# Attention, gate and hyena products in a fixed order on TensorE, with one bank for the projection and three for transposes and values

## The chip, the cores and the metric

The kernel runs on one core of a Trainium2 chip. The metric is the time of one execution in microseconds (us), the median of the runs shown. TensorE (PE) multiplies matrices into PSUM, which has 8 banks of 512 fp32 columns per partition. VectorE (DVE) and ScalarE (ACT) do the elementwise work, each in the order of its queue. SyncE (SP) and GpSimd (POOL) issue most DMAs.

## The reference

One layer of a diffusion backbone on 1024 tokens of width 1024, with 256 context tokens. One projection feeds two mixers, a neighbourhood attention (8 heads of 64) and a Hyena long convolution; their outputs are merged through sigmoid gates. Then come an output projection, a gated residual and a SwiGLU FFN. All six gates and shifts come from one vector (adaLN).

```python
h = modulate(rmsnorm(x, norm1_g[i]), sh1, sc1)
q, k, v, hv, hx1, hx2, gna, ghy = jnp.split(h @ w_in[i], IN_SPLITS, axis=-1)
y_na = neighbourhood_attention(to_heads(q), to_heads(k), to_heads(v), to_heads(k_c), to_heads(v_c), na_rpb[i])
y_hy = hyena_mixer(hv, hx1, hx2, *hy_params)
x = x + g1 * gated_merge(gna, ghy, y_na, y_hy, w_na_o[i], w_hy_o[i], w_out[i])
h2 = modulate(rmsnorm(x, norm2_g[i]), sh2, sc2)
x = x + g2 * swiglu(h2, ffn_w1[i], ffn_w3[i], ffn_w2[i])
# gated_merge:  m = sigmoid(g_na) * (y_na @ w_na_o) + sigmoid(g_hy) * (y_hy @ w_hy_o);  m @ w_out
```

Attention takes, for each query, a window of 8 rows by 16 columns of the 16 x 64 grid and all context keys, with a relative-position bias.

## The kernel before, in words

Products that need fp32 precision are made of three fp32r products: each operand is split into a high part (a cast, L174 on ACT) and a low part (a subtraction, L175 on DVE), and `gemm` (L186) adds low x high, high x low and high x high over the chunks of the contraction.

**The projection.** `project` (L552) makes the 40 chunks of `h @ w_in`, each of 128 output columns. A chunk has two halves of 512 tokens, a half is 24 matmuls of 128x512 into a tile in_ps (L560), so there are 80 halves. The last 16 chunks are the gates: ACT evicts each half with a sigmoid (L593) and POOL stores the chunk (L610). The weights of the next chunk are loaded and split ahead (wr, wh, wl).

**The convolution** runs beside the projection. Its last step transposes the result on PE in groups of four (yh_ps, L533; one bank, one buffer), ACT copies each group to yhT (L534), and POOL stores it.

**The attention** starts when the convolution is done (`self.fine`, L920). It has 32 items: a pair of heads, half the rows, a quarter of the columns. For an item:
- `scores` (L702): 12 matmuls into two tiles s_ps of two banks (two buffers), with operands krh, krl, kch, kcl, qh, ql, qrh, qrl. DVE adds the bias and takes the maximum (L728) into s, ACT makes the exponential into pe with its sum (L730), DVE takes the reciprocal and scales (L733, L734).
- `turn` (L737): five transposes of pe on PE into a tile pt_ps of two banks (L740), and a copy of 640 columns to pts by ACT (L742). An item calls it twice, once a head.
- `values` (L745): ten matmuls of v with pts into the unused columns of the pt_ps tile of the first head (L752), and a copy of 128 columns to yrow (L757).

An item's `turn` comes one step after its scores, its `values` two steps after. `keys` (L671) and `queries` (L693) load and prepare the operands of a pair: loads on SP (kraw, qraw, kcraw), a shuffle and rotary products on DVE, casts on ACT and subtractions on DVE. They are called in bursts at steps 1, 3 and 5 of the eight steps of a pair.

**Order.** Nothing here is pinned to program order: a scheduler places each instruction on its engine by its own estimate of when it is ready, and the generators' merge (`_merged`, with ATT1 = 23 steps of the attention beside the rest of the projection) only sets the order in which they are written. A half is written in three pieces (k 0-2, 3-5, 6-7) so that attention can come between. in_ps has two banks, in turn. PSUM: two banks in_ps, four s_ps, two pt_ps.

**After the last half** the projection's banks become ps1 (two banks), which hy_ps and al_ps share. `hyena_out` (L797) loads the convolution's result (yhraw, eight loads into two buffers), splits it (yhh, yhl), and makes 16 halves of 12 matmuls (hy_ps). DVE multiplies each by the stored gate (ghy, L816, in the buffers that yhraw used). `ada_late` (L836) sums the adaLN parts on PE (al_ps) from loads acc. Attention goes on beside them. Then `mix` begins with the attention's output product (na_ps).

Of the kernel before, what the change touches and what calls it, by code (L numbers as in the profile page):

```python
# [18 lines left out]
P = 128  # L19
D = 1024  # L20
T = 1024
# [3 lines left out]
ATT1 = 23  # L25
# [133 lines left out]
class Block:  # L159
# [26 lines left out]
    def gemm(self, ps, w, x, nk, width=512, pos=0, ks=None):  # L186

        nc = self.nc
        (wh, wl), (xh, xl) = w, x
        for k in ks or range(nk):  # L190
            for i, (ww, xx) in enumerate(((wl, xh), (wh, xl), (wh, xh))):
                nc.tensor.matmul(ps, ww[:, k * P:(k + 1) * P], xx[:, k, pos:pos + width],  # L192
                                 start=(k == 0 and i == 0), stop=(k == nk - 1 and i == 2))
# [358 lines left out]
    def project(self, groups, wpool, psg, psc, hT, hcT, between):  # L552

        nc = self.nc
        chunks = [f for g in groups for f in g]
        turn = []

        def half(f, w, st, ps, h):
            sl = slice(h * 512, (h + 1) * 512)
            pt = psg.tile([P, 512], F32, tag="g", name="in_ps")  # L560
            ps.append(pt)
            if self.fine:
                for ks in ((0, 1, 2), (3, 4, 5)):
                    self.gemm(pt, w, hT, 8, 512, h * 512, ks)
                    yield
                self.gemm(pt, w, hT, 8, 512, h * 512, (6, 7))
            else:
                self.gemm(pt, w, hT, 8, 512, h * 512)
# [50 lines left out]
        for group in groups:  # L619
# [7 lines left out]
            for h in range(2):  # L627
                for f, w, st, ps in zip(group, ws, sts, pss):
                    yield from half(f, w, st, ps, h)
# [11 lines left out]
    def attention(self, pool, kpool, prep, pss, pst):  # L641

        nc, a = self.nc, self.a
        rope = [kpool.tile([P, T], F32, name=f"rope{j}") for j in range(2)]
# [3 lines left out]
        nbias = 3  # L648
# [22 lines left out]
        def keys(pr):  # L671
# [9 lines left out]
            tl = {"v": v, "vc": vc, "q": [], "qr": []}  # L681
# [5 lines left out]
            for h in range(2):  # L687
                sl = slice(512 * h, 512 * h + 512)
                _, x = turned("k", self.qkd[4 + pr], sl, False)
                self.split(tl["kr"][0][:, sl], tl["kr"][1][:, sl], x)  # L690
            tiles[pr] = tl

        def queries(pr, h):  # L693

            for nm, x in zip(("q", "qr"), turned("q", self.qkd[pr], slice(512 * h, 512 * h + 512), True)):
                q = [prep.tile([P, 512], F32R, tag=nm + n, name=nm + n, bufs=2) for n in "hl"]
                self.split(*q, x)
                tiles[pr][nm].append(q)

        grid = lambda t, b: t[b:b + 64].rearrange("p (r c) -> p r c", c=64)  # L700

        def scores(it, pr, rb, cb):  # L702
# [15 lines left out]
            for i, (qq, kk) in enumerate(order):  # L718
                for ps, _, qs, _, kw, _ in halves:
                    nc.tensor.matmul(ps[:, 512:896], qs[qq], kw[kk], start=(i == 0), stop=(i == 2))  # L720
            for i, (qq, kk) in enumerate(order):
                for ps, _, _, qc, _, kc in halves:
                    nc.tensor.matmul(ps[:, 256:512], qc[qq], kc[kk], start=(i == 0), stop=(i == 2))  # L723
            pes = []
            for ps, bt, *_ in halves:
                s = pool.tile([P, 640], F32, tag="s", name="s", bufs=2)
                mx = pool.tile([P, 4], F32, tag="mx", name="mx", bufs=8)
                nc.vector.tensor_tensor_reduce(s, ps[:, 256:896], bt, -1.0, 3e38, ALU.add, ALU.min, mx[:, 0:1])  # L728
                pe = pool.tile([P, 640], F32, tag="pe", name="pe", bufs=4)
                nc.scalar.activation(pe, s, AF.Exp, bias=mx[:, 0:1], scale=-1.0, accum_out=mx[:, 1:2])  # L730
# [6 lines left out]
        def turn(pe):  # L737
            pt = pst.tile([P, T], F32, tag="t", name="pt_ps")
            for c in range(5):
                nc.tensor.transpose(pt[:, c * P:(c + 1) * P], pe[:, c * P:(c + 1) * P], self.ident)  # L740
            pts = pool.tile([P, 640], F32, tag="pts", name="pts", bufs=3)
            nc.scalar.copy(pts, pt[:, 0:640])  # L742
            return pts, pt

        def values(pts, yp, pr, rb, cb):  # L745

            tl = tiles[pr]
            for c in range(5):
                vv = tl["vc"][:, c, :] if c < 2 else tl["v"][:, 4 * (rb + c - 2) + cb, :]
                for hh in range(2):  # L750
                    ch = slice(64 * hh, 64 * hh + 64)
                    nc.tensor.matmul(yp[ch, 640:768], vv[:, ch], pts[hh][:, c * P:(c + 1) * P], start=(c == 0),  # L752
                                     stop=(c == 4), tile_position=(0, 64 * hh))
# [3 lines left out]
            nc.scalar.copy(dst, yp[:, 640:768].rearrange("p (r c) -> p r c", c=16))  # L757

        items = [(pr, rb, cb) for pr in range(4) for rb in range(2) for cb in range(4)]
        keys(0)  # L760
        queries(0, 0)
        yield
        one, two = {}, {}
        for it in range(len(items) + 2):
            if it < len(items):
                pr, at = it // 8, it % 8
                one[it] = scores(it, *items[it])
                if at == 1:
                    queries(pr, 1)
                elif at == 3 and pr < 3:  # L770
                    keys(pr + 1)
                elif at == 5 and pr < 3:
                    queries(pr + 1, 0)
            p0, p1 = one.pop(it - 1, (None, None))
            if p0 is not None:
                pts, yp = turn(p0)
                two[it - 1] = [pts]
            else:
                yp = pst.tile([P, T], F32, tag="t", name="pt_ps")
# [3 lines left out]
            if p1 is not None:  # L783
                two[it - 1].append(turn(p1)[0])
# [12 lines left out]
    def hyena_out(self, pool, wo, ps1):  # L797
# [10 lines left out]
        for f in range(8):  # L808
            w = self.weights(wo, a["why"][f], 512, "wf")
            for h in range(2):  # L810
                sl = slice(h * 512, (h + 1) * 512)
                ps = ps1.tile([P, 512], F32, tag="f", name="hy_ps")
                self.gemm(ps, w, yh, 4, 512, h * 512)
# [22 lines left out]
    def ada_late(self, pool, psf, part, gate):  # L836

        nc = self.nc
        for h in range(2):
            sl = slice(h * 512, (h + 1) * 512)  # L840
            acc = pool.tile([P, 512], F32, tag="acc", name="acc")
            nc.sync.dma_start(acc, self.accd[part][:, sl])
            ps = psf.tile([P, 512], F32, tag="f", name="al_ps")
            if gate is not None:
# [547 lines left out]
```

## Time and profile before

| | us |
|---|---|
| median of 3 runs (lowest, highest) | 1765.49 (1762.91, 1771.47) |
| the profiled execution | 1768.11 |
| its span | 1766.3 |
| mean granted clock of TensorE | 0.979 |
| first scores of the attention | 687.21 |
| last half of the projection ends, next item's scores | 848.32 |
| first matmul of na_ps | 965.26 |

The span runs from the first to the last instruction of the profiled execution. A row of a timeline has the start, the duration, engine, line and operation, the tiles written and read, the shapes, and in brackets how long the engine idled before it and what it waited for. The durations of matmuls overlap on PE, so a matmul's cost is read from start to start. "<-issue" is a wait that the profile names no releaser for. The clock column is 1.00 at full speed and 0.50 at half.

### The profile page before, as it was taken

The numbers are of one execution on the slowest core, as the hardware profiler recorded it, in microseconds if no ns is written. First come the engines' busy times: TensorE is split into PE (matmuls) and PEld (weight loads), VectorE is DVE, ScalarE is ACT, GpSimd is POOL, SyncE is SP. The second block draws the span as 40 slices with busy tenths as digits, with TensorE's granted clock in tenths as the row PEclk, the third lists the DMA queues.
The fourth block names the chain that finished last, engine by engine and source line by source line (L and its number), as shares of the span: only waits on it lengthen the run. The fifth ranks groups of instructions, "written<-read, shape, count | busy, mean of one in ns | idle before, by whom it ended". The sixth has DMA issues, their size and how long they took to land.

```text
span 1766.3 us, 22607 instructions
## 1 busy us (share of the span) xinstructions
PE 1687.7 (96%) x8128; PEld 1325.4 (75%) x8128; DVE 1226.2 (69%) x2040; ACT 693.0 (39%) x1190; POOL 142.8 (8%) x250
## 2 busy tenths in 40 slices
PE   6999899999999998999999999899999999999997
PEld 2777676777777776777677788688888888878886
DVE  4587487799797856856645867887656656469466
ACT  4611122312212124777734214633334333344555
POOL 0000010101100014022000000001100000100000
PEclk8999999999999998999999999999999999999999
DMA  8276756645455338444556624242322332395344
GB/s 339 106 245 196 233 191 209 224 143 182 137 205 184 135 120 212 122 141 124 171 181 202 228 77 167 92 153 103 135 92 90 102 107 96 112 370 167 101 120 150
DMA packets 111469, 285.36 MB, mean 162 GB/s; under 512 B 14707, under 2 KB 23543, under 8 KB 109053
## 3 DMA queue, kind: packets, MB, share of 16 engines
q1 hardware_dynamic: 91888, 221.32, 38.4%
q0 software_dynamic: 18816, 62.14, 10.2%
q8 instruction: 65, 1.06, 0.3%
q10 hardware_dynamic: 653, 0.44, 0.1%
q14 instruction: 47, 0.39, 0.1%
HBM read 213.86 MB, written 69.99 MB: 161 GB/s over the span
## 4 chain that ended last, share of the span: by engine, by line
PE 54%; issue 26%; DMA 8%; DVE 6%; ACT 2%; POOL 2%; SPq 0%; POOLq 0%; DVEq 0%; ACTq 0%
PE in_ps L192 18%; PE dx_ps L1261 6%; PE dft_ps L420 4%; PE out_ps L1041 3%; PE dz_ps L1261 3%; PE x_ps L1103 2%; DMA wal<-in_w_ada 2%; PE dft_ps L421 2%; PE dft_ps L422 2%; PE na_ps L192 2%; PE hy_ps L192 2%; PE pt_ps L752 2%; PE dy_ps L1261 2%; PE pt_ps L740 2%; POOL g L1214 1%
## 5 line engine op out<-in xcount | busy, mean ns | idle before, releaser
L192 PE MATMUL in_ps<-hTh,wl 128*128 128x512 f32 x640 | 260.4, 408 | 0.0
L192 PE MATMUL in_ps<-hTl,wh 128*128 128x512 f32 x640 | 255.7, 400 | 0.0
L192 PE MATMUL in_ps<-hTh,wh 128*128 128x512 f32 x640 | 254.3, 398 | 0.0
L192 PEld LDWEIGHTS in_ps<-hTl,wh 128*128 128x128 f32 x640 | 121.9, 191 | 27.3 <-issue 3.7
L192 PEld LDWEIGHTS in_ps<-hTh,wl 128*128 128x128 f32 x640 | 122.0, 191 | 26.0 <-issue 1.3
L192 PEld LDWEIGHTS in_ps<-hTh,wh 128*128 128x128 f32 x640 | 122.0, 191 | 25.9 <-issue 0.8
L175 DVE TENSOR_TENSOR ol<-ws,oh 128x512 fp32r<-128x512 f32 x88 | 60.2, 688 | 58.4 <-ACT oh L174 58.3
L174 ACT CAST wh<-wr 128x1024 fp32r<-128x1024 f32 x40 | 41.9, 1049 | 117.1 <-PE in_ps L192 88.3
L175 DVE TENSOR_TENSOR ol<-ar,oh 128x512 fp32r<-128x512 f32 x77 | 52.9, 687 | 46.1 <-ACT oh L174 46.1
L175 DVE TENSOR_TENSOR wl<-wr,wh 128x1024 fp32r<-128x1024 f32 x40 | 48.8, 1220 | 46.0 <-ACT wh L174 45.9
L174 ACT CAST oh<-ar 128x512 fp32r<-128x512 f32 x77 | 47.9, 622 | 81.8 <-PE dx_ps L1261 36.3
L420 PE MATMUL dft_ps<-a,matf 128*128 128x512 f32 x128 | 66.5, 601 | 7.1 <-issue 3.7
L174 ACT CAST oh<-ws 128x512 fp32r<-128x512 f32 x88 | 54.3, 622 | 47.7 <-PE x_ps L1103 16.4
L1261 PE MATMUL dx_ps<-ol,oh 128*128 128x512 f32 x176 | 69.6, 396 | 1.7 <-DVE ol L175 1.7
L1261 PE MATMUL dx_ps<-oh,ol 128*128 128x512 f32 x176 | 67.5, 392 | 3.7 <-ACT oh L174 3.5
L832 DVE SCALAR_TENSOR_TENSOR aacc<-wal,cs,aacc 128x1024 f32<-128x1024 f32 x32 | 41.0, 1282 | 41.9 <-DMA wal<-in_w_ada 41.0
L1261 PE MATMUL dx_ps<-oh 128*128 128x512 f32 x176 | 69.5, 395 | 0.0
L728 DVE CUSTOM_DVE_ANT_0 s<-s_ps,bias 128x640 f32<-128x640 f32 x64 | 50.6, 819 | 25.0 <-PE s_ps L723 24.9
L174 ACT CAST oh<-wr 128x512 fp32r<-128x512 f32 x70 | 43.2, 621 | 53.2 <-PE y_ps L1103 18.2
L175 DVE TENSOR_TENSOR ol<-wr,oh 128x512 fp32r<-128x512 f32 x70 | 48.0, 688 | 23.0 <-ACT oh L174 22.9
L742 ACT COPY pts<-pt_ps 128x640 f32<-128x640 f32 x64 | 44.2, 691 | 48.0 <-PE pt_ps L740 47.2
L1043 DVE TENSOR_TENSOR x<-x,out_ps 128x512 f32<-128x512 f32 x64 | 42.6, 684 | 19.3 <-PE out_ps L1041 18.9
(390 smaller groups left out, 4312.9 us busy)
## 6 DMA issues: line engine op xcount, KB each, us to landing
wr<-in_w SPq DMA_DIRECT2D x50, 512.0 KB, 3.3
wr<-in_w_in SPq DMA_DIRECT2D x40, 512.0 KB, 4.3
ar<-g SPq DMA_DIRECT2D x77, 256.0 KB, 2.9
wal<-in_w_ada SPq DMA_DIRECT2D x32, 512.0 KB, 4.1
g<-t POOLq DMA_DIRECT2D x49, 256.0 KB, 3.1
matf<-in_dft_f SPq DMA_DIRECT2D x32, 384.0 KB, 4.7
bias<-in_rpb SPq DMA_DIRECT2D x64, 192.0 KB, 2.9
w<-in_w SPq DMA_DIRECT2D x44, 256.0 KB, 5.4
```

What stands on the lines that cost most here:

```text
L174: self.nc.scalar.copy(hi, src)
L175: self.nc.vector.tensor_sub(lo, src, hi.bitcast(F32))
L192: nc.tensor.matmul(ps, ww[:, k * P:(k + 1) * P], xx[:, k, pos:pos + width], start=(k == 0 and i == 0), stop=(k == nk - 1 and i == 2))
L420: nc.tensor.matmul(ps, m[:, 0], v.rearrange("p a b -> p (a b)"), start=True, stop=False)
L421: nc.tensor.matmul(ps[:, 0:256], m[:, 1], v[:, 1], start=False, stop=False)
L422: nc.tensor.matmul(ps[:, 256:512], m[:, 2], v[:, 0], start=False, stop=True)
L728: nc.vector.tensor_tensor_reduce(s, ps[:, 256:896], bt, -1.0, 3e38, ALU.add, ALU.min, mx[:, 0:1])
L742: nc.scalar.copy(pts, pt[:, 0:640])
L832: nc.vector.scalar_tensor_tensor(acc, w, self.cs[:, 2 * k:2 * k + 1], acc, op0=ALU.mult, op1=ALU.add)
L1041: nc.tensor.matmul(ps, gg[x][:, tk], ww[y][:, sl], start=(i == 0), stop=(i == n - 1))
L1043: nc.vector.tensor_add(x1[:, sl], x1[:, sl], ps)
L1261: nc.tensor.matmul(ps[j], x[u][:, j * P:(j + 1) * P], w[v], start=(start and i == 0 and c == 0), stop=(stop and i == N - 1 and k == len(re ...
```

## The change

It sets the order of PE's instructions in this stage by hand and moves buffers and banks accordingly.

- `gemm` takes `pin`; with it every matmul keeps its place in program order (`keep_in_program_order`). The halves of the projection in this stage, scores, transposes of pe, values, hyena halves and al_ps are all pinned.
- A half is written in one piece. in_ps has two pools of one bank each, and in this stage only the first is used: one bank. The bank that is saved goes to pt_ps, which now has three banks and one buffer: ten transposes in columns 0 to 1279, values in 1280 to 1407. One copy of 1280 columns replaces two of 640.
- A step is written as scores of item i, ten transposes of item i-1, values of item i-2. Five units of the projection stand ahead of the first step, then one step and one half in turn.
- `operands()` prepares one piece (a quarter or so of a pair's operands) at every step, not in bursts. Bias tiles: four, not three. The reduction writes straight into pe, and the exponential is in place.
- After the last half: ps1 has one bank, hy_ps is pinned, `ada_late` is one generator over the parts 3, 4, 2, 5, and the steps of attention, hyena and al are interleaved by the step's number.

```diff
-    def gemm(self, ps, w, x, nk, width=512, pos=0, ks=None):
+    def gemm(self, ps, w, x, nk, width=512, pos=0, pin=False):
...
+                if pin:
+                    self.tc.keep_in_program_order(mm)
...
-            pt = psg.tile([P, 512], F32, tag="g", name="in_ps")
+            pt = psg[0 if self.fine else count[0] % 2].tile([P, 512], F32, tag="g", name="in_ps")
             ps.append(pt)
-            if self.fine:
-                for ks in ((0, 1, 2), (3, 4, 5)):
-                    self.gemm(pt, w, hT, 8, 512, h * 512, ks)
-                    yield
-                self.gemm(pt, w, hT, 8, 512, h * 512, (6, 7))
-            else:
-                self.gemm(pt, w, hT, 8, 512, h * 512)
+            self.gemm(pt, w, hT, 8, 512, h * 512, self.fine)
...
+        def operands():
+
+            values_of(0)
+            yield from keys(0)
+            yield from queries(0, 0)
+            for pr in range(4):
+                yield from queries(pr, 1)
+                if pr < 3:
+                    values_of(pr + 1)
+                    yield from keys(pr + 1)
+                    yield from queries(pr + 1, 0)
...
-                s = pool.tile([P, 640], F32, tag="s", name="s", bufs=2)
+                pe = pool.tile([P, 640], F32, tag="pe", name="pe", bufs=4)
...
-                nc.vector.tensor_tensor_reduce(s, ps[:, 256:896], bt, -1.0, 3e38, ALU.add, ALU.min, mx[:, 0:1])
...
+                nc.vector.tensor_tensor_reduce(pe, ps[:, 256:896], bt, -1.0, 3e38, ALU.add, ALU.min, mx[:, 0:1])
+                nc.scalar.activation(pe, pe, AF.Exp, bias=mx[:, 0:1], scale=-1.0, accum_out=mx[:, 1:2])
...
+        def turn(pes, pt):
+            for n, pe in enumerate(pes):
+                for c in range(5):
+                    at = 640 * n + c * P
+                    pin(nc.tensor.transpose(pt[:, at:at + P], pe[:, c * P:(c + 1) * P], self.ident))
+            pts = pool.tile([P, 2, 640], F32, tag="pts", name="pts", bufs=2)
+            nc.scalar.copy(pts.rearrange("p a b -> p (a b)"), pt[:, 0:1280])
+            return pts
...
+            pt = pst.tile([P, 1536], F32, tag="t", name="pt_ps")
+            if it - 1 in one:
+                two[it - 1] = turn(one.pop(it - 1), pt)
             if it >= 2:
-                values(two.pop(it - 2), yp, *items[it - 2])
+                values(two.pop(it - 2), pt, *items[it - 2])
...
-                for _ in _merged((proj, 6 * self.left), (attention, ATT1)):
-                    if not self.left:
-                        break
+                next(attention)
+                for _ in range(AHEAD):
+                    next(proj)
+                while self.left:
+                    next(attention)
+                    next(proj)
...
-                    ps1 = E4(tc.tile_pool(name="ps1", bufs=2, space=PSUM))
+                    ps1 = E4(tc.tile_pool(name="ps1", bufs=1, space=PSUM))
...
+                    for n, _ in enumerate(attention):
+                        if n > 2 and n % 4 != 3 or n in (3, 19):
+                            next(hyena, None)
+                        if n % 2:
+                            next(late, None)
```

What this does to the order, at three places. The first is ACT's queue from the convolution's last copy (yhT) into the attention. Each proj<-in_ps is the eviction of one half; kch, krh, qh and qrh are casts of the attention's operands, wh one of weights. Before:

```order
L534 COPY yhT_4956<-yh_ps_4963 128x512
L593 ACTIVATE proj_4977<-in_ps_4978 128x512
L174 CAST kch_5047<-kcraw_5045 128x256
L174 CAST wh_5151<-wr_5149 128x1024
L593 ACTIVATE proj_4977<-in_ps_5091 128x512
L174 CAST krh_5043<-kraw_5051 128x512
L593 ACTIVATE proj_5155<-in_ps_5156 128x512
L174 CAST krh_5043<-kraw_5060 128x512
L174 CAST qh_5073<-qraw_5069 128x512
```

After, from the same place:

```order
L539 COPY yhT_4959<-yh_ps_4966 128x512
L174 CAST kch_5060<-kcraw_5058 128x256
L594 ACTIVATE proj_4980<-in_ps_4981 128x512
L174 CAST krh_5056<-kraw_5064 128x512
L174 CAST wh_5126<-wr_5124 128x1024
L174 CAST krh_5056<-kraw_5073 128x512
L174 CAST qh_5086<-qraw_5082 128x512
L594 ACTIVATE proj_4980<-in_ps_5097 128x512
L174 CAST qrh_5093<-qraw_5082 128x512
L174 CAST qh_5276<-qraw_5272 128x512
L594 ACTIVATE proj_5130<-in_ps_5131 128x512
```

The evictions of the first two halves, which stood ahead of kch and of both krh, now stand behind kch and behind both krh and qh. Further on, not shown, the fourth half's follows kch, qrh and wh, and the fifth's two krh of the next pair.

The second place is PE in the middle of the attention. Before, one item's scores with what stands between them (in_ps the projection, pt_ps from ident the transposes, from v and vc the values):

```order
L192 MATMUL in_ps<-hTh,wh 128x512
L720 MATMUL s_ps<-krh,qrl 128x384 x2
L720 MATMUL s_ps<-krl,qrh 128x384 x2
L720 MATMUL s_ps<-krh,qrh 128x384 x2
L752 MATMUL pt_ps<-pts,vc 64x128 x4
L752 MATMUL pt_ps<-pts,v 64x128 x6
L723 MATMUL s_ps<-kch,ql 128x256 x2
L723 MATMUL s_ps<-kcl,qh 128x256 x2
L740 MATMUL pt_ps<-ident,pe 128x128 x5
L723 MATMUL s_ps<-kch,qh 128x256 x2
L192 MATMUL in_ps<-hTh,wl 128x512
```

After, an item there:

```order
L194 MATMUL in_ps<-hTh,wh 128x512
L739 MATMUL s_ps<-krh,qrl 128x384 x2
L739 MATMUL s_ps<-krl,qrh 128x384 x2
L739 MATMUL s_ps<-krh,qrh 128x384 x2
L742 MATMUL s_ps<-kch,ql 128x256 x2
L742 MATMUL s_ps<-kcl,qh 128x256 x2
L742 MATMUL s_ps<-kch,qh 128x256 x2
L759 MATMUL pt_ps<-ident,pe 128x128 x10
L771 MATMUL pt_ps<-pts,vc 64x128 x4
L771 MATMUL pt_ps<-pts,v 64x128 x6
L194 MATMUL in_ps<-hTh,wl 128x512
```

The item is one block, and the next rows are the 24 matmuls of a half without a break. From the first scores to the last projection matmul PE changes between projection, scores, transposes and values 145 times before and 44 times after; from there to na_ps 98 and 86 times (hyena and al counted as kinds as well). In the first of these stretches stand 320 projection matmuls, 21 items' scores, 200 transposes and 190 value matmuls before, and 288, 12, 110 and 100 after; what is missing there comes in the second, where before has 11 items' scores, 120 transposes and 130 value matmuls, and after 20, 210 and 220. Ahead of the first scores, the sixteen transposes yh_ps follow each other without a break after; before, 13, 4 and 4 projection matmuls stood between their groups. Behind them come 144 projection matmuls after, 90 before.

The third place is ACT behind the last half's eviction. Before, up to the second yhh (the cast of the convolution's result from its load yhraw):

```order
L730 ACTIVATE pe_7041,mx_7039<-s_7038,mx_7039 128x640
L730 ACTIVATE pe_7046,mx_7044<-s_7043,mx_7044 128x640
L757 COPY yrow_6734<-pt_ps_7067 128x8x16
L174 CAST yah_6977<-yrow_5291 128x512
L174 CAST yah_6977<-yrow_6013 128x512 x2
L174 CAST yah_6977<-yrow_6734 128x512
L174 CAST yhh_6988<-yhraw_6990 128x512
L174 CAST yhh_6988<-yhraw_6994 128x512
```

After:

```order
L761 COPY pts_6420<-pt_ps_6409 128x1280
L174 CAST wfh_6625<-wfr_6623 128x512
L174 CAST wfh_6794<-wfr_6792 128x512
L174 CAST yhh_6343<-yhraw_6345 128x512
L174 CAST yhh_6343<-yhraw_6349 128x512
L776 COPY yrow_6203<-pt_ps_6409 128x8x16
L748 ACTIVATE pe_6453,mx_6454<-pe_6453,mx_6454 128x640
L174 CAST yhh_6343<-yhraw_6353 128x512
L174 CAST yhh_6343<-yhraw_6357 128x512
```

The first yrow copy in this stretch stood ahead of the first yhh and now stands behind two of them; the next ones (not shown) stand behind the sixth and the eighth. On PE, al_ps follows directly behind a hyena half at the steps 3, 5, 9 and 13 behind the last half.

More of the change, by code (lines that the diff above doesn't have):

```diff
@@ L735, in scores, with values @@
             return [pe for pe, _ in pes]
[L737 to L745, printed above, removed]
+        def turn(pes, pt):
[6 more added lines that the diff above has]
+            return pts
+        def values(pts, pt, pr, rb, cb):
             tl = tiles[pr]
@@ L756, in values @@
             dst = self.yrow[pr].rearrange("p (r c) -> p r c", c=64)[:, 8 * rb:8 * rb + 8, 16 * cb:16 * cb + 16]
[L757 removed]
+            nc.scalar.copy(dst, pt[:, 1280:1408].rearrange("p (r c) -> p r c", c=16))
         items = [(pr, rb, cb) for pr in range(4) for rb in range(2) for cb in range(4)]
[L760 to L761 removed]
+        prepared = operands()
+        for _ in range(6):
+            next(prepared)
         yield
```

124 lines of the change are left out of this document (62 added, 62 removed).

## The prediction

> **What bounds the kernel now.** I read the page's head first, then busy time by stage, then what TensorE (PE) waits for in the stage that the change rewrites, then single instructions of that stage.
>
> ```profile
> span 1766.3 us, 22607 instructions
> PE 1687.7 (96%) x8128; PEld 1325.4 (75%) x8128; DVE 1226.2 (69%) x2040; ACT 693.0 (39%) x1190; POOL 142.8 (8%) x250
> ```
>
> The profiled execution took 1768.11 us, 2.6 above the median of the three timed runs (1765.49). PE is busy for 96% of the span, so two things can shorten the kernel: fewer PE microseconds, or less of the little idle time. The instructions up to the last transform of the convolution (641 us) and those from the mixing stage on (965.3 us, the first na_ps) stand in the same order on PE in both kernels. I therefore work on the 324 us between, in three pieces.
>
> ```profile
> 641.00:688.00 47.00, 39.55 (x183) 32.16 (x183) 29.24 (x47) 12.36 (x20) 15.30 (x28) 0.95 0.70 203
> 688.00:850.00 162.00, 160.20 (x1167) 123.48 (x1164) 108.92 (x255) 125.72 (x211) 29.79 (x53) 0.98 0.45 133
> 850.00:965.50 115.50, 106.10 (x730) 80.29 (x729) 63.00 (x140) 55.80 (x113) 8.69 (x16) 0.96 0.60 192
> 965.50:1766.30 800.80, 778.70 (x3412) 637.38 (x3411) 551.50 (x873) 329.39 (x584) 46.03 (x85) 0.99 0.41 138
> ```
>
> Columns: length, then busy time of PE, its weight loads, DVE, ACT and POOL, the granted clock, DMA share, GB/s. PE's idle time is 7.45 us in the start, 1.8 in the middle and 9.4 in the late piece. There is little to win by removing waits. Who causes them:
>
> ```profile
> PE s_ps L720 <- issue: 7.5, 1, 7.5
> PE pt_ps L740 <- ACT pts L742: 3.0, 2, 2.2
> PE s_ps L720 <- DVE mx L728: 2.8, 4, 1.6
> ```
>
> Columns: total, times, longest. The largest is the first item's scores, which wait from the end of a projection matmul (679.8) for their prepared operands. These two rows and the first of na_ps bound the pieces:
>
> ```profile
> 679.37 0.39 PE L192 MATMUL in_ps<-hTh,wl 128*128 128x512 f32 x1
> 687.21 0.69 PE L720 MATMUL s_ps<-krh,qrl 64*128 64x384 f32 x2 [7.45 <-issue]
> 965.26 0.50 PE L192 MATMUL na_ps<-yah,wfl 128*128 128x512 f32 x1 [0.36 <-ACT yrow L757]
> ```
>
> **The prices.** A steady item of before, on PE:
>
> ```profile
> 838.75 0.44 PE L720 MATMUL s_ps<-krh,qrl 64*128 64x384 f32 x2
> 839.84 0.77 PE L740 MATMUL pt_ps<-ident,pe 128*128 128x128 f32 x5
> 840.36 0.47 PE L192 MATMUL in_ps<-hTh,wl 128*128 128x512 f32 x1
> 840.68 0.39 PE L192 MATMUL in_ps<-hTl,wh 128*128 128x512 f32 x1
> ...
> 841.13 0.40 PE L192 MATMUL in_ps<-hTh,wl 128*128 128x512 f32 x1
> 841.72 0.66 PE L752 MATMUL pt_ps<-pts,vc 128*64 128x128 f32 x8 [0.20 <-ACT pts L742]
> 842.97 0.50 PE L192 MATMUL in_ps<-hTl,wh 128*128 128x512 f32 x1
> 848.32 0.45 PE L720 MATMUL s_ps<-krh,qrl 64*128 64x384 f32 x2
> ```
>
> From start to start: the scores of an item (12 matmuls) 1.09 us; five transposes 0.52, so ten 1.04; the ten value products 842.97 - 841.72 = 1.25; a projection matmul 0.23 (two in 841.13 - 840.68; 24 of a half: 5.5); and the first one after another kind 0.32, so a change of kind costs 0.09. The item took 848.32 - 838.75 = 9.57 us.
>
> **Part 1, fewer changes of kind.** By count of the two orders, from the first scores to the last projection matmul there are 145 changes of kind before and 44 after; from there to na_ps 98 and 86. That is 113 x 0.09 = 10.2 us off PE. The item bears it out roughly: 9.57 less 0.20 of wait and 8.90 for the pieces leaves 0.47 for its seven changes, 0.07 each. Bounds: nothing (if the gap only moves) and 10.2.
>
> **Part 2, the start: one bank for in_ps.** In this stage every half of a chunk (24 matmuls) now uses the same bank. Half n+1 can't begin until ACT has evicted half n (the sigmoid). ACT runs in order, and in its new order these evictions stand behind casts of the attention's operands (kch, krh, qh, qrh), which wait for loads and for DVE. Before, two banks, and evictions between those casts, kept PE running. The casts' times in before:
>
> ```profile
> 654.58 1.22 DVE L522 SCALAR_TENSOR_TENSOR yo<-yo,hx 128x1024 f32<-128x1024 f32 x1
> 659.36 0.59 ACT L534 COPY yhT<-yh_ps 128x512 f32<-128x512 f32 x1 [0.75 <-PE yh_ps L533]
> 667.91 0.41 ACT L174 CAST kch<-kcraw 128x256 fp32r<-128x256 f32 x1 [5.12 <-DMA kraw<-qk]
> 673.99 0.62 ACT L174 CAST krh<-kraw 128x512 fp32r<-128x512 f32 x1 [4.22 <-DVE kraw L668]
> 681.36 0.62 ACT L174 CAST qh<-qraw 128x512 fp32r<-128x512 f32 x1 [2.70 <-DMA qraw<-qk]
> 692.90 0.41 ACT L174 CAST kch<-kcraw 128x256 fp32r<-128x256 f32 x1 [2.61 <-DMA kcraw<-kc]
> ```
>
> The sixteen transposes of the convolution's result (yh_ps) come first and are now consecutive, in one bank: the second four wait for DVE (655.8), the last go out near 659.0, as the copy at 659.36 shows for before. Before, 13 + 4 + 4 projection matmuls (21 x 0.23 = 4.8 us) ran between them; now PE idles that long. Then, with loads and DVE where they were, six halves run (numbered from 1 here). Half 1 runs 659.1 to 664.6; its eviction follows kch (668.3), so half 2 runs 669.0 to 674.5. That eviction follows two krh, a weight cast and qh (681.4 + 0.6), so half 3 begins at 682.5. It would take 5.5 us, and 1.7 more if the clock halves for 3.4 us (below): 689.7. Half 4 runs 690.3 to 695.8. Its eviction follows kch (692.9), a qrh that waits for DVE and a weight cast: half 5 runs 697 to 702.5. Half 6 waits for two krh of the next pair; no row prices this order of them, I take 2 to 5 us: 705 to 710.5. So the first scores go out at 711 instead of 687.2. I keep 700 (all loads some 6 us sooner, half 3 held 5 less) and 716 as ends.
>
> **Part 3, the middle.** From the first scores to the last half, before takes 687.2 to 848.3, 161.1 us. Off it go 1.8 idle and 3.2 half clock (2% of 162, by the clock column): 156.1 of work. After has 32 projection matmuls (7.4), 9 items' scores (9.8), 90 transposes (9.4) and 90 value products (11.3) fewer here, and 101 changes (9.1): 109.1 us. An item takes about 9.1 us of PE. What hides the eviction of the single bank is the block of scores, transposes and values behind each half, 1.09 + 1.04 + 1.25 = 3.4 us against a table load and a sigmoid:
>
> ```profile
> 693.33 1.28 ACT L730 ACT_TABLE_LOAD   x1
> 694.62 0.83 ACT L730 ACTIVATE pe<-s,mx 128x640 f32<-128x640 f32 x1
> 848.42 0.60 ACT L593 ACTIVATE proj<-in_ps 128x512 f32<-128x512 f32 x1 [0.48 <-PE in_ps L192]
> 838.75:848.32 9.57, 8.04 (x12) 1.00 0.15 44
> ```
>
> 1.28 + 0.60 = 1.9 fits, if nothing long stands ahead. The last row is ACT alone over that item: 8.04 busy of 9.57, so ACT fits into 9.1 as well. The two copies of 640 columns that become one of 1280, and the operand unit per item, leave its sum about the same. The half ends the middle at 711 + 109.1 = 820.1. I take no new idle time here; the bound is the rival on ACT. The scores written straight into pe cost nothing: same DVE and ACT instructions, with the four pe tiles enough for two items.
>
> **Part 4, the late piece.** Nine more items fall behind the last half, with nothing of the projection to cover them, next to the loads and casts of yhraw for the hyena product. Work: 117.0 us before (848.3 to 965.3), less 9.4 idle and 4.6 half clock (4% of 115.5), is 103.0; plus 9 items 30.5, less 12 changes 1.1: 132.4. Waits: the probabilities' transposes and values now share one tile (three banks, one buffer), so the transposes of item i+1 wait for the yrow copy of item i-1. In ACT's new order these copies stand behind casts of yhraw, which wait for loads into two buffers.
>
> ```profile
> 857.13 1.17 ACT L174 CAST yhh<-yhraw 128x512 fp32r<-128x512 f32 x2 [0.90 <-DMA yhraw<-yh]
> 861.42 0.62 ACT L174 CAST yhh<-yhraw 128x512 fp32r<-128x512 f32 x1
> 875.66 0.62 ACT L174 CAST yhh<-yhraw 128x512 fp32r<-128x512 f32 x1 [2.10 <-DMA yhraw<-yh]
> ```
>
> The first pair is cast 8.7 us after the last sigmoid, which the loads wait for; the next starts 4.3 later. Four pairs by that pace are done 8.7 + 3 x 4.3 + 1.2 = 22.8 us after the half, and the fourth transposes go out near 24. PE has 3 x 1.04 + 3 x 1.25 + 4 x 1.09 and some changes and small matmuls, 13 us, ahead of them: 11 us idle (bounds: 5, for the first pair alone, and 15, at the last cast's 27.3). Second, hy_ps and al_ps now share one bank, and in four iterations al stands right behind a hyena half, behind the DVE product (ghy) that frees the bank.
>
> ```profile
> L816 DVE TENSOR_TENSOR ghy<-hy_ps,ghy 128x512 f32<-128x512 f32 x16 | 11.1, 691 | 28.8 <-PE hy_ps L192 20.2 <-PE al_ps L849 4.5 <-DMA ghy<-gate 2.1
> ```
>
> The product itself is 0.69 us (mean 691 ns). At the first of the four DVE has eight operand instructions of such a length queued ahead of it, some 5.5 us. I take 5 there and 6 for the rest (bounds 3 and 15). Together 22 us of idle time, ends 8 and 30. Half clock comes on top:
>
> ```profile
> 893.00:894.00 1.00, 0.00 (x0) 1.00 0.59 158
> 894.00:895.00 1.00, 0.53 (x2) 0.91 0.61 201
> 895.00:896.00 1.00, 1.00 (x8) 0.50 0.94 268
> 897.00:898.00 1.00, 1.00 (x12) 0.50 0.33 115
> ```
>
> After about 1.6 us without a matmul (PE column 0, then 0.53) the clock is 0.50 for some 3.4 us, so such a gap costs up to 1.7 us more. Two or three of the gaps lead to that: 4 us (0 to 8). The Trainium skill, "TensorE: Matmul & The Clock Gate", in its part on the clock gate, puts the half rate behind at least one idle window of about 3.4 us. By it the shorter gaps would cost nothing extra and this term would be about 2 us lower; the row above disagrees, and the sum goes by the row.
>
> **The sum.** 820.1 + 132.4 + 22 + 4 = 978.5 for na_ps, against 965.3: 13.2 us later. Everything behind it is unchanged. In the profile's scale 1768.1 + 13.2 = 1781.3, beside the median 1765.5 + 13 = 1778.5.
>
> **The rivals.** *The late casts don't hold PE.* In before ACT has half its late time free (55.8 of 115.5) and the first copies might slip past the loads sooner; the new order's strict place speaks against it. With 8 us of waits and half clock instead of 26 the sum is 5 us below before: 1760, within the noise. Chance 0.20.
>
> *Faster: the loads land sooner.* The casts that hold the evictions wait for loads issued while the queues were full:
>
> ```profile
> 676.11 3.63 SPq L658 DMA_DIRECT2D qraw<-qk  x2
> ```
>
> ```profile
> 678.00:679.00 1.00, 1.00 (x6) 1.00 1.06 371
> ```
>
> At a DMA share of 1.06 (sixth number; PE's clock is the fifth) the qraw load took from 676.1 to 681.4. If weights and values leave the queues to the operands, each arrives some 6 us sooner, the first scores go out at 700, and the same in the yhraw loads leaves 10 us of late waits: 700 + 109.1 + 142.4 = 951.5, 14 us earlier, 1752. It decides from qh cast before about 677. For it: PE asks for weights later. Against: kraw and its predecessors, rope and bias, stand in SP's queue as before. Chance 0.17.
>
> *Slower still: ACT is the bound of the middle.* If two table loads an item cost more than their rows, or the queue idles between, the twelve items stretch from 9.1 to 10 us: 11 more, 1789. Against: the rows above, where the exponential starts 0.01 us after the table load ends. Chance 0.08. The Trainium skill, "ScalarE: Activation LUTs", in its part on what the table load costs, says that a switch takes 2.66 us, 1.38 of it a drain. By it, ACT's 8.04 would be 10.8 and this rival would hold; the 0.01 us shows no drain here.
>
> **How the numbers follow.** The forecast has 0.55. About 0.5% (8.8 us) is what a measurement of this kernel can tell from no change. Faster by more: nearly all of the second rival and a little of the first, 0.18. Within: the rest of the first, and the forecast's low end (a start at 707, late waits of 18): 0.26. Slower: 0.56. The range takes the forecast's own ends (1765 to 1794), the first rival and most of the third and second: 1755 to 1797.
>
> **What would show it.** Right: PE idle over 15 us between 655 and 715, released by ACT's sigmoid; items of about 9.1 us; waits of pt_ps for yrow and of al_ps for ghy in the 40 us behind the last half; na_ps near 978. Wrong: first scores before 703, no wait of in_ps for its eviction, or items over 9.6 us.

## The result and the profile after

The changed kernel took 1884.74 us (median of 4 runs, 1881.11 to 1888.4), the kernel before 1768.48 beside it (4 runs). The ratio is 1.064, with a 95% interval of 1.0612 to 1.0667: about 115 us slower, where I had forecast 13 slower and a range up to 1797. The direction was right and the size was not.

The head of the page, then the stages of the changed kernel, cut at its own first scores, at the scores behind its last half and at its first na_ps (columns as before: length, busy time of PE, weight loads, DVE, ACT and POOL, clock, DMA share, GB/s):

```profile
span 1879.2 us, 22516 instructions
PE 1714.4 (91%) x8128; PEld 1354.1 (72%) x8128; DVE 1230.5 (65%) x2041; ACT 686.4 (37%) x1154; POOL 142.9 (8%) x250
```

```profile
641.00:712.83 71.83, 56.64 (x221) 43.44 (x219) 41.41 (x68) 16.68 (x27) 22.18 (x40) 0.88 0.61 180
712.83:858.13 145.30, 117.77 (x744) 94.61 (x743) 59.55 (x135) 83.22 (x119) 13.16 (x23) 0.92 0.28 87
858.13:1079.36 221.23, 160.78 (x1123) 127.16 (x1123) 106.41 (x241) 90.59 (x166) 18.72 (x33) 0.85 0.41 130
1079.36:1879.20 799.84, 777.88 (x3412) 637.58 (x3412) 551.00 (x872) 327.22 (x581) 46.50 (x86) 0.99 0.40 137
```

The first scores go out at 712.83 (forecast 711), and the time behind na_ps is the same as before (799.8 and 801). All that I missed is in the two rows between: the middle takes 145.3 us, not 109.1, and the late piece 221.2, not 158.4. PE stands idle there for 27.5 and 60.5 us, and the clock is 0.92 and 0.85. What PE waits for, over the whole run:

```profile
PE pt_ps L771 <- ACT pts L761: 80.9, 31, 4.3
PE in_ps L194 <- ACT proj L594: 11.4, 6, 4.6
```

One wait fills the first row: the value matmuls (L771) for a copy pts (L761), 31 times, 2.6 us each. It is in no line of my sum. One item on PE, and ACT at the same time:

```profile
780.49 0.28 PE L742 MATMUL s_ps<-kch,qh 64*128 64x256 f32 x2
780.70 1.31 PE L759 MATMUL pt_ps<-ident,pe 128*128 128x128 f32 x10
783.85 0.66 PE L771 MATMUL pt_ps<-pts,vc 128*64 128x128 f32 x8 [1.84 <-ACT pts L761]
```

```profile
782.09 0.60 ACT L594 ACTIVATE proj<-in_ps 128x512 f32<-128x512 f32 x1
782.58 1.22 ACT L761 COPY pts<-pt_ps 128x1280 f32<-128x1280 f32 x1
783.82 1.28 ACT L748 ACT_TABLE_LOAD   x1
```

The ten transposes end near 782.0. ACT copies what they wrote from 782.58 to 783.80, and only at 783.85 do the value matmuls begin. Yet these values belong to the item before: their probabilities were copied a whole item earlier. What they wait for is the copy of the transposes that stand directly ahead of them, and it stands behind a table load and a sigmoid on ACT. In the next item it stands behind two exponentials, and the wait is 3.96 us.

### The profile page after: what moved, and what is told of

Same layout as the page of the kernel before. It is cut to its first block, busy times and chain, and to the rows that moved or that the text cites. A ratio compares the mean times of both kernels' runs of the same rounds, so it can differ in the third digit from the quotient of the medians.

```text
span 1879.2 us, 22516 instructions
## 1 busy us (share of the span) xinstructions
PE 1714.4 (91%) x8128; PEld 1354.1 (72%) x8128; DVE 1230.5 (65%) x2041; ACT 686.4 (37%) x1154; POOL 142.9 (8%) x250
## 4 chain that ended last, share of the span: by engine, by line
PE 30%; issue 19%; ACT 6%; DVE 4%; DMA 3%; POOL 2%; SPq 0%; POOLq 0%; ACTq 0%; DVEq 0%
PE dx_ps L1284 5%; PE in_ps L194 5%; PE out_ps L1064 3%; PE dz_ps L1284 3%; PE hy_ps L194 3%; PE pt_ps L771 3%; ACT pe L748 2%; PE na_ps L194 2%; PE x_ps L1126 2%; ACT pts L761 2%; PE dy_ps L1284 2%; POOL g L1237 1%; POOL g L1231 1%; PE s_ps L739 1%; PE z_ps L1126 1%
## 5 line engine op out<-in xcount | busy, mean ns | idle before, releaser
L194 PE MATMUL in_ps<-hTh,wl 128*128 128x512 f32 x640 | 264.6, 414 | 11.4 <-ACT proj L594 11.4
L771 PE MATMUL pt_ps<-pts,vc 128*64 128x128 f32 x256 | 24.9, 324 | 80.9 <-ACT pts L761 80.9
L747 DVE CUSTOM_DVE_ANT_0 pe<-s_ps,bias 128x640 f32<-128x640 f32 x64 | 50.2, 821 | 68.3 <-PE s_ps L742 68.3
L771 PEld LDWEIGHTS pt_ps<-pts,vc 128*64 128x64 f32 x256 | 15.6, 154 | 88.9 <-ACT pts L761 88.6
L748 ACT ACTIVATE pe<-pe,mx 128x640 f32<-128x640 f32 x64 | 52.5, 821 | 45.5 <-DVE mx L747 45.3
L174 ACT CAST oh<-wr 128x512 fp32r<-128x512 f32 x70 | 43.2, 621 | 53.4 <-PE y_ps L1126 18.2
```

Of the source, the lines that this page charges most:

```text
L174: self.nc.scalar.copy(hi, src)
L194: mm = nc.tensor.matmul(ps, ww[:, k * P:(k + 1) * P], xx[:, k, pos:pos + width], start=(i == 0), stop=(i == n - 1))
L747: nc.vector.tensor_tensor_reduce(pe, ps[:, 256:896], bt, -1.0, 3e38, ALU.add, ALU.min, mx[:, 0:1])
L748: nc.scalar.activation(pe, pe, AF.Exp, bias=mx[:, 0:1], scale=-1.0, accum_out=mx[:, 1:2])
L771: pin(nc.tensor.matmul(pt[ch, 1280:1408], vv[:, ch], pts[:, hh, c * P:(c + 1) * P], start=(c == 0), stop=(c == 4), tile_position=(0, 64 * ...
```

## The experiments

All kernels are the changed kernel with the edit shown. Two theories were open. A: the values wait because they write into the tile that the copy reads. B: ACT as a whole can't keep up with the items in this order, and the wait would turn up elsewhere.

### Values ahead of the transposes

```diff
+            if it >= 2:
+                values(two.pop(it - 2), pt, *items[it - 2])
             if it - 1 in one:
                 two[it - 1] = turn(one.pop(it - 1), pt)
             if it >= 2:
-                values(two.pop(it - 2), pt, *items[it - 2])
+                keep(pt, *items[it - 2])
                 self.pairs_done(*items[it - 2])
```

`keep` is the yrow copy, which stood at the end of `values`.

> The changed kernel with one thing moved: the ten value matmuls of item i-2 stand ahead of the ten transposes of item i-1, in the same pt_ps tile; the yrow copy is written behind the transposes. Theory A: in the changed kernel the values wait for the pts copy of the transposes right ahead of them (80.9 us in 31 waits), because they write into a bank which that copy reads, not for their own data; moved ahead, they need only the copy of a step before. Then the 80.9 us go, and with the gaps most of the half clock (about 25 us), while the late waits for yrow, ghy and casts that I had forecast (22 + 4 us) can come out: na_ps near 980 instead of 1079, time 1775 to 1800. Rival B: ACT as a whole is too slow for the items, so the wait goes to the transposes or to the next values: 1850 or more.

Measured: 1771.22 us, 4 below the range of theory A, a ratio to before of 1.0018 (0.9999 to 1.0038). The whole loss of the change goes with this one exchange. Stages, cut in the same way:

```profile
641.00:712.26 71.26, 55.60 (x215) 42.72 (x213) 40.96 (x68) 15.43 (x25) 22.25 (x40) 0.88 0.62 181
712.26:817.88 105.62, 105.07 (x743) 86.80 (x742) 58.99 (x135) 82.61 (x119) 13.45 (x23) 1.00 0.38 118
817.88:972.49 154.61, 136.44 (x1123) 110.53 (x1123) 104.87 (x241) 88.65 (x166) 18.73 (x33) 0.93 0.61 191
```

Over middle and late piece PE's idle time falls from 27.53 + 60.45 = 88.0 us to 0.55 + 18.17 = 18.7, which is 69.3 less; its busy time falls from 278.6 to 241.5, which is 37.0 less for as many matmuls, because the clock is higher. That is the 106 us by which na_ps comes sooner. ACT's busy time in the middle is the same in both (83.2 and 82.6), in 145 and in 106 us: B falls. ACT has time for the items; only the copy comes too late for values that stand right behind the transposes. The 80.9 us of waits are more than the 69.3 because 11.6 us of other waits, for yrow, yhh and ghy, come out behind the last half when the items run faster.

### A half of the projection between transposes and values

```diff
+            half_between = self.left > 0
+            if half_between:
+                yield
             if it >= 2:
                 values(two.pop(it - 2), pt, *items[it - 2])
                 self.pairs_done(*items[it - 2])
-            yield
+            if not half_between:
+                yield
```

> The changed kernel with a half of the projection (24 matmuls) between an item's transposes and the values behind them, as long as there are halves; late piece as in the changed kernel. Theory A: the copy has 5.5 us instead of none, so the middle's waits (30.5 of the 80.9 us) and its half clock (about 10) go, the late 50 stay: time 1840 to 1850. Rival B (ACT too slow as a whole): the middle stays at about 153 us and the time at 1880.

Measured: 1851.13 us (one run), 1 above the range of theory A. The waits that are left:

```profile
PE pt_ps L771 <- ACT pts L761: 50.7, 21, 2.9
PE in_ps L194 <- ACT proj L594: 11.4, 7, 5.3
```

All 21 lie behind the last half; while there are halves to put between, no value matmul waits for the copy. In the middle of the changed kernel the values waited 1.84 to 4.34 us for it, and the 5.5 us of a half hide that. The scheduler had done the same in the kernel before, with single projection matmuls.

### No shared bank, and then no shared tile

To tell the bank from the tile I left two of ten transposes out, so that the values have the third bank for themselves:

```diff
-                for c in range(5):
+                for c in range(5 - 2 * n):
...
-            nc.scalar.copy(pts.rearrange("p a b -> p (a b)"), pt[:, 0:1280])
+            flat = pts.rearrange("p a b -> p (a b)")
+            nc.scalar.copy(flat[:, 0:1024], pt[:, 0:1024])
+            nc.scalar.copy(flat[:, 1024:1280], pt[:, 768:1024])
```

> The changed kernel with eight transposes instead of ten (two of the second head left out, its last 256 columns of pts filled from others), so that the third bank of pt_ps holds values alone and no copy reads it; order, tile and length of the copies about as before. If the wait comes from the shared bank: the values' waits go though they still stand behind the transposes, and the time is near that of values first (1770 to 1800, 7 us of transposes left out). If it comes from the shared tile, or from the values' own data: 70 us or more of waits stay and the time is over 1850.

Measured: 1921.06 us (one run), with

```profile
PE pt_ps L773 <- ACT pts L763: 101.8, 31, 5.1
```

The values still wait, now for the second of the two copies, though neither copy touches their bank. So it is not the bank. The next kernel differs from this one in the tile alone (the columns of the values and of their yrow copy move with it, not shown):

```diff
-            pt = pst.tile([P, 1536], F32, tag="t", name="pt_ps")
+            pt = pst.tile([P, T], F32, tag="t", name="pt_ps")
+            yp = pst.tile([P, 512], F32, tag="y", name="yp_ps")
...
-                values(two.pop(it - 2), pt, *items[it - 2])
+                values(two.pop(it - 2), yp, *items[it - 2])
```

> As the third run (eight transposes, two left out, values behind the transposes, two copies of pts), but the values write into a tile of their own, of one bank, and the transposes' tile has two banks: the same banks hold the same things, only the tile is another. If the wait comes from the shared tile, of which any part being read by a copy holds the next matmul into any other part: the third run's 101.8 us of waits go, and the time is 1765 to 1800. If it is the values' own data or their place behind the transposes: waits of 70 us or more stay, over 1850.

Measured: 1773.23 us (one run), 148 us less than with the shared tile. In this run the values follow the transposes at once, with the copy still to come, and no value matmul of the run waits for a copy any more:

```profile
781.61 1.09 PE L759 MATMUL pt_ps<-ident,pe 128*128 128x128 f32 x8
782.64 0.66 PE L773 MATMUL yp_ps<-pts,vc 128*64 128x128 f32 x8
```

```profile
783.49 1.01 ACT L762 COPY pts<-pt_ps 128x1024 f32<-128x1024 f32 x1
```

So the wait hangs on the tile: in these kernels a matmul into one part of the tile is held until copies that were written earlier in the program have read other parts of it. The columns of values and copy never overlapped. As the same matmuls and copies ran beside each other with two tiles in banks of their own, the wait of the third run is one that the program sets, not one that the chip needs. For the changed kernel itself that is not shown: its copy also reads 256 columns of the values' bank, and no run here tests whether a copy can read a bank while PE writes into it. Which step of the program's building sets the wait, these runs don't show either.

### The start, and the late piece

Values first stands level with before. What still costs it is what I had forecast, the start and the late piece. The first try lends in_ps two free banks at the start:

```diff
+            if self.fine and self.borrowed < 5:
+                self.borrowed += 1
+            if self.fine and self.borrowed in (1, 2, 4) and self.lend is not None:
+                pt = self.lend.tile([P, T], F32, tag="s", name="in_ps")[:, 0:512]
+            else:
+                pt = psg[0 if self.fine else count[0] % 2].tile([P, 512], F32, tag="g", name="in_ps")
```

> Values first, and three of the first five halves of the projection write into banks of s_ps, which are free until the first scores, so that in_ps has three banks at the start. Theory: the first scores at 712.8 us in the changed kernel are late because each half waits for the eviction of the one before, behind casts on ACT; with the banks they go out at about 698, and the time is 10 to 15 us below values first. Rival: the scores wait for their operands anyway and PE has the same halves to do: within 3 us of values first.

Measured: 1768.19 us, ratio 1.0003 (0.998 to 1.0027), against 1.0018 (0.9999 to 1.0038) of values first: no difference that can be told. The first scores went out at 706.5, not 698: one wait of 7.7 us for an eviction was left. The theory failed. The next two kernels put three units of the projection ahead of the scores (AHEAD = 3, not 5), without the lent banks and with them:

> Values first, and three units of the projection ahead of the first scores, not five: four halves there, and two more items covered by halves later. Theory: the start loses its time to halves that each wait for an eviction (first scores at 712 us, PE idle some 15 us before them); two of these halves moved behind the first scores are evicted in the cover of the blocks, so the first scores go out near 699, and the time is 5 to 8 us below values first. Rival: the scores then wait for operands instead: within 2 us of values first.

> The fourth run (values first, banks lent at the start) with three units of the projection ahead, not five, two halves in lent banks. Theory: that run's longest wait (7.7 us, the fifth half on the third's eviction) goes, the first scores go out at 692 to 696, and the time is 6 to 10 us below values first, some 5 below before. Rival: the wait goes to the operands, as before's own 7.5 us: within 2 us of the fourth run.

Measured: 1779.62 (1.0059, 1.0039 to 1.008) and 1777.93 us (1.0045, 1.0026 to 1.0064). The first scores did go out sooner, at about 695 in both, and yet the sixth run is slower than values first and the seventh slower than the fourth: the theory of the start was right about the scores and wrong about the time. The gain was given back behind the last half, where the sixth run takes 156.5 us with two items fewer to do, and values first 154.6. There the seventh waits for

```profile
PE al_ps L876 <- DVE ghy L838: 8.7, 2, 7.3
PE hy_ps L194 <- DVE ghy L838: 5.0, 3, 3.4
PE pt_ps L780 <- ACT yrow L787: 3.8, 3, 2.0
PE na_ps L194 <- DVE ghy L838: 3.7, 1, 3.7
```

Fewer steps were left behind the last half, so three hyena halves stood in a row before na_ps, each on the one bank that DVE must free. I tried two remedies. The first begins hyena later, one half a step:

```diff
-                        if n > 2 and n % 4 != 3 or n in (3, 19):
+                        if n > 4:
                             next(hyena, None)
```

> The seventh run with the hyena halves beginning two steps later behind the last half of the projection (from the fifth step on, one a step). Theory: behind the last half, values first waits some 12 us for yrow, yhh, yhl and ghy between 826 and 851 us, because hyena starts before its operands are cast; two steps later most of the yhh, yhl and ghy part (about 8) goes: 4 to 8 us below the seventh run. Rival: the yrow copies behind the casts hold the items just the same, and the hyena halves end later: within 2 us of it.

Measured: 1770.88 us (0.9997, 0.9976 to 1.0017), 7 below the seventh run, as expected. Its trace bears the reason out only in part: waits behind the last half are 19.9 us against 25.2, but na_ps comes only 1.1 us sooner, the seventh's profiled execution (1772.87) being the fastest of its ten and the eighth's (1773.34) among its slowest. The second puts al_ps ahead of the hyena half of its step and leaves none at the end, on the seventh run (hyena from the fourth step) and on the fourth (from the sixth):

```diff
-                        if n > 2 and n % 4 != 3 or n in (3, 19):
-                            next(hyena, None)
                         if n % 2:
                             next(late, None)
+                        if n > 2:
+                            next(hyena, None)
```

> The seventh run with one hyena half at every step from the fourth on (so that no three of them stand in a row at the end) and al_ps ahead of the hyena half of its step, not right behind it. Theory: the seventh run got its first scores 11 us earlier than the fourth and lost it behind the last half: al behind a hyena half in the shared bank (8.7 us), three hyena halves in a row on one bank before na_ps (8.7). Both go: 8 to 14 us below the seventh run, 1764 to 1770. Rival: the late piece is held by the loads and casts of yhraw and by half clock whatever stands there: within 3 us of the seventh run, 1775 to 1781.

> The fourth run (values first, lent banks, five units ahead) with al_ps ahead of the hyena half of its step, and the hyena halves from the sixth step on, one a step. Theory: its waits of al and hyena for ghy and yhh behind the last half (10.5 us, and the half clock that they bring) mostly go: 5 to 12 us below the fourth run, 1757 to 1763, faster than before. Rival: as in the eighth run, what goes there comes back as waits of the items for yrow: within 3 us of the fourth run.

Measured: 1762.26 us (0.9945, 0.9923 to 0.9968) and 1762.47 us (0.9962, 0.9944 to 0.998). Both are faster than before, by 0.55% and 0.38%, and than the changed kernel; the first is 2 us below its forecast range, the second inside. The late piece of the seventh run and of the ninth, cut in the same way:

```profile
819.00:973.20 154.20, 129.03 (x1040) 104.66 (x1039) 100.02 (x226) 82.16 (x154) 18.28 (x33) 0.92 0.62 195
```

```profile
816.16:958.07 141.91, 125.97 (x1039) 101.78 (x1039) 96.39 (x223) 79.71 (x152) 18.56 (x33) 0.96 0.62 191
```

Idle time falls from 25.2 to 15.9 us and half clock with it. Of the 15.1 us by which na_ps comes sooner here, 3.1 lie ahead of the first scores, which the edit doesn't touch. In the tenth run the time came as forecast, but not for the reason given. The waits of al and hyena for ghy and yhh went, yet PE's idle time behind the last half is no smaller than in the fourth run (17.8 us against 16.8): waits of hyena on al's copies (5.1 us for g, 3.7 for mod) and of values for yrow (6.3) took their place. What fell there is half clock (0.95 against 0.91), which makes the piece 3.8 us shorter; another 4.1 us were won ahead of the first scores, which the edit doesn't touch. Why the tenth run is faster is therefore open in part.

## Why the prediction was wrong

**The step that failed** is the pricing of the shared tile in part 4, and "I take no new idle time here" in part 3. I wrote that transposes and values share one tile with one buffer, and drew one wait from it: the transposes of item i+1 for the yrow copy of item i-1. The other direction, the values for the pts copy of the transposes just ahead of them, I priced at nothing without naming it, though the change puts the two side by side in every item. It cost 80.9 us of waits and some 37 of half clock, less the 11.6 of other waits that they hid.

**The row that carried it** stood in my own quotation of before: the values at 841.72, "[0.20 <-ACT pts L742]". I took its 0.20 us off the item's time and did not ask what the values waited for. ACT at that place in before:

```profile
840.47 0.60 ACT L593 ACTIVATE proj<-in_ps 128x512 f32<-128x512 f32 x1
840.98 0.69 ACT L742 COPY pts<-pt_ps 128x640 f32<-128x640 f32 x1
```

Five transposes end at 840.61, four projection matmuls follow, the copy ends at 841.67, and the values of another item start at 841.72. The wait of 0.20 us was the uncovered rest of one of about 1.1, and the projection matmuls between were its cover. I counted their removal as a gain (fewer changes of kind) and did not ask what they hid.

**Start**: right in what it waits for, and in its time partly by luck. First scores came at 712.83 against 711, five of the halves released by the eviction of the one before, at 672.5, 684.2, 693.3, 700.7 and 707.2 us against 669.0, 682.5, 690.3, 697 and 705. The transposes of the convolution's result came out 4 us later than I took them. The waits of these five halves were 10.8 us where my schedule has 16.7, and half clock took some 8.6 us (0.88 over 71.83 us) where it has 1.7; the two errors nearly cancel.

**Changes of kind and the middle**: right once the values are moved. An item then takes

```profile
781.71 0.45 PE L739 MATMUL s_ps<-krh,qrl 64*128 64x384 f32 x2
...
790.75 0.45 PE L739 MATMUL s_ps<-krh,qrl 64*128 64x384 f32 x2
```

9.04 us (forecast 9.1, before 9.57), and the middle 105.6 (109.1).

**The late piece**: with values first 154.6 us against 158.4, but the terms differ: 18.2 idle against 22, and more half clock (0.93 over the piece, against 4 us in my sum). In the changed kernel itself hardly any of it showed, since the items came more slowly than the casts: its waits for ghy and yrow there are 6.5 us. These waits appear only when the larger one goes. The sum that I made comes near values first: na_ps at 972.49 against 978.5, and 2 us above before (1771.22 beside 1769.25) against 13.

**The rivals**: ACT as the bound of the middle did not hold; ACT had 83 us of work in 145. (The 8.04 us by which I had weighed it hold three table loads, at 839.17, 841.69 and 846.66, not the two that I reckoned with.) The faster rival (loads that land sooner) did not come: the first scores stayed at 712, and the qh cast came at 683.00, not before 677. That the late casts don't hold PE was true of the changed kernel, for another reason than I gave.

## What to carry to other kernels

When a change removes work between two instructions of one engine, look for what that work hid: find the second instruction's releaser in the trace, even where the wait in brackets is small, and price the wait without the cover, clock included. In these kernels a matmul into a tile waits for copies of other parts of that tile that the program wrote ahead of it, so put the writer that needs only old data first, or give it a tile and a bank of its own. A wait that is removed brings out the next one: in the sixth and seventh runs the first scores came 17 us sooner than with values first, which was to make the time 5 to 10 us shorter, and nothing of it arrived until the hyena and al steps at the end were placed anew.

## What the runs showed of the hardware that was not expected

Half clock followed gaps of well under 3 us, but not every one. Between 713 and 1000 us of the changed kernel PE had nine gaps of 2.55 or 2.56 us; five brought a stretch at 0.50 of 3.4 us and four none. Two of them alike, by microsecond (length, busy, clock, DMA share, GB/s), the first with the gap ending at 821.75, the second at 956.45:

```profile
820.00:821.00 1.00, 0.00 (x0) 1.00 0.80 203
821.00:822.00 1.00, 0.25 (x4) 1.00 0.46 168
822.00:823.00 1.00, 1.00 (x16) 0.59 0.03 8
823.00:824.00 1.00, 1.00 (x9) 0.50 0.00 0
824.00:825.00 1.00, 1.00 (x3) 0.50 0.35 131
825.00:826.00 1.00, 1.00 (x4) 0.71 0.31 90
826.00:827.00 1.00, 1.00 (x6) 1.00 0.40 107
```

```profile
954.00:955.00 1.00, 0.00 (x0) 1.00 0.68 177
955.00:956.00 1.00, 0.00 (x0) 1.00 0.97 322
956.00:957.00 1.00, 0.55 (x10) 1.00 0.84 244
957.00:958.00 1.00, 1.00 (x16) 1.00 0.15 55
958.00:959.00 1.00, 1.00 (x6) 1.00 0.09 16
```

Of the four gaps of 1.84 us there, one brought it. My rule in the prediction, half clock after about 1.6 us, was too simple: what decides is where a gap falls. The clock column gives the moment of each change: 0.59 in the row from 822 and 0.71 in the row from 825 put the drop at 822.18 and the rise at 825.58. All 44 changes found in this way between 658 and 1065 us of this trace lie a whole number of steps of 3.413 us behind the drop at 658.33, to within 0.03 us. The first gap (819.19 to 821.75) lies inside one step of this grid, 818.76 to 822.17, and the clock drops at its end. The second (953.89 to 956.45) is cut by the bound at 955.29 into 1.40 and 1.16 us, and no drop follows.

Among the steps at full clock, each of the 20 with 1.86 us or more without a matmul ended in a drop, one of the three with 1.84 us, and none with 1.79 us or less. This bound holds for this trace alone. Less was enough in values first, 1.25 us with eight al_ps matmuls of two columns beside it (drop at 869.52), and twice in before: 1.60 us with the same matmuls beside it, in the row that my rule came from, and 1.49 us with transposes and scores (drop at 857.27). So the kind of work in a step seems to count as well, which no run here tests by itself. Half clock cost 37 us more than with values first, beside 80.9 us of waits.

The Trainium skill, "TensorE: Matmul & The Clock Gate", in its part on the clock gate, gives at least one idle window of about 3.4 us as the condition; here steps that were idle for 1.86 us brought it, so the measurement differs. The same part says that the window runs freely and doesn't start anew with the kernel; the grid of this trace agrees with a window that runs freely.
